# Seven rooms instead of four for gathered expert rows in the dense part

## The chip, the cores and the metric

One NeuronCore of a Trainium2 chip runs the whole kernel as one program. The metric is the device time of one execution in microseconds; for the kernel before, the median of 3 runs is 3912.84 us (3907.16 to 3918.35). The profile is that of one further execution.

## The reference

The kernel computes one decoder block on 1024 tokens of width 1024, in float32. Time mixing and a sparse attention come first; the change touches only the last layer, a product-key expert layer (PEER). Each token picks 128 of 16384 experts (8 heads of 16), with a gate for each. Every expert has a row of 1024 numbers in a table u and one in a table v:

```python
def chunk(args):
    hc, ec, gc = args
    act = jax.nn.gelu(jnp.einsum('cd,chkd->chk', hc, u_tab[ec]), approximate=False) * gc
    return jnp.einsum('chk,chkd->cd', act, v_tab[ec])
```

A residual addition and a layer norm follow and give the output rows.

## The kernel before

The expert layer is done in two ways at once. The last 576 tokens are done **densely**: the dot products of all these tokens with all 16384 experts are formed on TensorE, multiplied by a table of gates that is zero where a token did not pick an expert, and multiplied with v. The first 448 tokens are done by **gather**: for each of their picks the row of u, and later the row of v, is fetched from HBM by an indirect DMA, and VectorE does the arithmetic.

**Dense part.** It starts where the pools of the retrieval close, at the mark `dense`. For 128 groups of 128 experts, `dense_u` forms dot products (or reads those formed earlier back from HBM into `al`), applies GELU on ScalarE, multiplies by the gates `gt` on VectorE (L1317) and splits the product in a high and a low half (L1319) in a tile `A`. `dense_v` multiplies eight such tiles with a tile of v and adds the result to `yacc` on VectorE (L1333). Each tile of u or v comes through `split2`: SyncE's queue loads 128x1024 floats (512 KB) into one of two buffers `raw` (L1270), ScalarE copies them to `whi`, rounded, and GpSimd subtracts to get `wlo` (L1274). I call one such subtraction a **split**. There are 264 of them in the program, numbered here in the order in which they stand on GpSimd, and 48 matrix products or so wait for each. A `raw` buffer is free for the next load when its split has ended.

**Gather.** `peer_gather` goes through 896 rows of work; a row is one indirect DMA that GpSimd issues (L1397), which brings 128x1024 floats (512 KB) into a **room**, and one pass of VectorE over it: L1401 for u (a dot product with the token), L1405 for v (a weighted sum in PSUM). There are four token tiles: three of 256 rows and one of 128 rows. After each, `finish` adds the residual, normalises and writes the output rows. A room is taken again only after VectorE has read it. Rows 1 to 128 use three rooms `g`; rows 129 to 300 (constants `EARLY` and `MIDDLE`) use three `g` and three `gx`; from row 301 on, in the dense part, the rooms are three `g` and `GM` rooms `g2`:

```python
if row >= MIDDLE and row % (GB + GM) >= GB:
    return at["dv"].tile([128, 1024], F32, name="g2", bufs=GM)
return grow()
```

**Order.** The gather's instructions are written last in the source, after the whole dense part. A scheduler merges them in when the program is built: it keeps a model of time, and moves a row forward to where its room is free in that model. The result is one fixed order for each engine; on the chip an engine takes its instructions in that order and waits at the first that is not ready. Rooms therefore decide two things: how many rows may be in flight, and where in the fixed orders of GpSimd and VectorE the rows stand.

Of the kernel before, what the change touches and what calls it, by code (L numbers as in the profile page):

```python
# [41 lines left out]
SQ = 6  # L42
XOB = 2
QIB = 2
GM = 1
FIRST = 3
XR = 3
TIES = 3
# [157 lines left out]
def body(tc, a, out, dbg=None, ntiles=8, mark=lambda s: None):  # L206
# [1129 lines left out]
    def grow(bufs=GB):  # L1336
        return gp.tile([128, 1024], F32, name="g", bufs=bufs)
# [20 lines left out]
    def peer_gather(i, at):  # L1358
# [11 lines left out]
        def room(row):  # L1370
            if EARLY <= row < MIDDLE and row % (GB + XR) >= GB:
                return at["sl"].tile([128, 1024], F32, name="gx", bufs=XR)
# [3 lines that stand above are left out]
# [394 lines left out]
```

## Time and profile before

| | |
|---|---|
| median of 3 runs | 3912.84 us (3907.16 to 3918.35) |
| profiled execution, its time | 3897.85 us |
| its span, first to last instruction | 3895.7 us |
| mean granted TensorE clock | 0.927 of full speed |
| TensorE matmul busy | 3364.8 us (86%) |
| VectorE busy | 2739.8 us (70%) |
| GpSimd busy | 2102.5 us (54%) |
| moved by DMA | 977.19 MB, mean 251 GB/s |

Shares of the whole span mix stages with different limits. Here the end of the program is two stages: the dense part from about 2350 us to about 3600 us, and what is left of the gather after it. The times in the views are microseconds from the start of the span.

### The profile page before, as it was taken

Reading aid. Unit: us, or ns where it says so; the run is one execution under the profiler, and the core shown is the slowest. Engines: PE = TensorE matmul, PEld = TensorE weight load, DVE = VectorE, ACT = ScalarE, POOL = GpSimd, SP = SyncE. Lnnn points to the kernel's source line nnn. Section 1 sums busy time; section 2 is a strip of 40 time slices with the busy share of each in tenths; the row PEclk is TensorE's granted clock in tenths of the full one; section 3 lists DMA queues with packets and bytes.
Section 4 is the critical chain, followed back from the end, with each engine's and each line's share of the span. In section 5 each row is a group of like instructions: output and inputs, shape, how many; then the busy total and the mean of one; then the engine's idle time right before and its main releaser. Section 6 shows DMA issues by size and latency. Waiting matters only on the chain. (4 is left out here: it accounts for less than half of the span.)

```text
span 3895.7 us, 65006 instructions
## 1 busy us (share of the span) xinstructions
PE 3364.8 (86%) x23921; PEld 2994.4 (77%) x23921; DVE 2739.8 (70%) x5625; ACT 1650.8 (42%) x3156; POOL 2102.5 (54%) x1702
## 2 busy tenths in 40 slices
PE   8999998799999999799999989999999999998000
PEld 7677776666777676588999989999999999997000
DVE  7866645856477758899999945666666666676776
ACT  3559842433444443455686683332323222222000
POOL 5442222355555543366565516767766777778554
PEclk9999998899999999899999989999999999998555
DMA  7453335756677665598888749889889888998886
GB/s 230 148 151 104 108 97 178 253 178 224 183 219 220 216 213 159 181 320 297 315 310 313 285 153 314 316 322 339 321 315 319 323 316 326 332 325 300 286 292 230
DMA packets 448418, 977.19 MB, mean 251 GB/s; under 512 B 42036, under 2 KB 190084, under 8 KB 445668
## 3 DMA queue, kind: packets, MB, share of 16 engines
q1 hardware_dynamic: 305060, 488.55, 37.7%
q0 software_dynamic: 143040, 484.50, 35.2%
q8 instruction: 188, 3.08, 0.3%
q14 instruction: 130, 1.06, 0.1%
HBM read 853.88 MB, written 119.01 MB: 250 GB/s over the span
## 5 line engine op out<-in xcount | busy, mean ns | idle before, releaser
L1274 POOL TENSOR_TENSOR wlo<-raw,whi 128x1024 fp32r<-128x1024 f32 x264 | 641.6, 2432 | 333.7 <-ACT whi L235 327.1
L416 POOL TENSOR_TENSOR wlo<-wraw,whi 128x512 fp32r<-128x512 f32 x280 | 370.4, 1325 | 553.8 <-ACT whi L235 511.5
L1397 POOL DMA_INDIRECT g<-in_u_dram,gidx x425 | 434.5, 1022 | 341.7 <-DVE g L1401 211.0
L1405 DVE SCALAR_TENSOR_TENSOR pg<-g,dots,pg 128x1024 f32<-128x1024 f32 x380 | 488.1, 1285 | 158.9 <-DMA g<-in_v_dram,gidx 146.9
L235 ACT ACTIVATE whi<-raw 128x1024 fp32r<-128x1024 f32 x264 | 279.1, 1058 | 632.5 <-PE pair L1289 263.6
L1287 PE MATMUL pair<-A,whi 128*128 128x288 f32 (+2 forms) x2048 | 460.3, 302 | 35.5 <-DVE A L1319 24.4
L1397 POOL DMA_INDIRECT g<-in_v_dram,gidx x384 | 365.8, 953 | 231.3 <-DVE pg L1405 128.3
L1401 DVE SCALAR_TENSOR_TENSOR g<-g,pg 128x1024 f32<-128x1024 f32 x297 | 358.3, 1216 | 161.4 <-DMA g<-in_u_dram,gidx 158.7
L1291 PE MATMUL pair<-h2T,wlo 128*128 128x288 f32 x2048 | 452.5, 301 | 17.2 <-POOL wlo L1274 17.2
L1287 PE MATMUL pair<-h2T,whi 128*128 128x288 f32 x2048 | 451.4, 301 | 18.3 <-ACT whi L235 18.1
L1291 PE MATMUL pair<-A,wlo 128*128 128x288 f32 (+2 forms) x2048 | 458.2, 301 | 4.8 <-POOL wlo L1274 4.8
L1289 PE MATMUL pair<-A,whi 128*128 128x288 f32 (+2 forms) x2048 | 458.4, 301 | 1.9 <-DVE A L1319 1.9
L1289 PE MATMUL pair<-h2T,whi 128*128 128x288 f32 x2048 | 447.7, 300 | 0.0
L1287 PEld LDWEIGHTS pair<-A,whi 128*128 128x128 f32 x2048 | 341.7, 193 | 39.1 <-issue 26.2
L426 PE MATMUL acc<-big,whi 128*128 128x512 f32 x864 | 354.6, 411 | 17.0 <-DVE zs L534 5.9
L1291 PEld LDWEIGHTS pair<-h2T,wlo 128*128 128x128 f32 x2048 | 335.6, 192 | 21.1 <-POOL wlo L1274 20.0
L1287 PEld LDWEIGHTS pair<-h2T,whi 128*128 128x128 f32 x2048 | 335.9, 192 | 20.7 <-ACT whi L235 19.1
L428 PE MATMUL acc<-big,wlo 128*128 128x512 f32 x864 | 349.4, 405 | 2.3 <-POOL wlo L416 2.3
L427 PE MATMUL acc<-big,whi 128*128 128x512 f32 x864 | 347.8, 403 | 1.4 <-DVE big L452 1.4
L1291 PEld LDWEIGHTS pair<-A,wlo 128*128 128x128 f32 x2048 | 341.6, 193 | 5.5 <-POOL wlo L1274 5.5
L1289 PEld LDWEIGHTS pair<-A,whi 128*128 128x128 f32 x2048 | 342.0, 193 | 2.5 <-DVE A L1319 2.5
L1289 PEld LDWEIGHTS pair<-h2T,whi 128*128 128x128 f32 x2048 | 335.8, 192 | 0.7
(489 smaller groups left out, 6632.0 us busy)
## 6 DMA issues: line engine op xcount, KB each, us to landing
raw<-in_vt_dram SPq DMA_DIRECT2D x136, 512.0 KB
raw<-in_ut_dram SPq DMA_DIRECT2D x128, 512.0 KB
wraw<-in_wz_dram SPq DMA_DIRECT2D x152, 256.0 KB
gtD<-st SPq DMA_DIRECT2D x18, 2048.0 KB
gt<-gtD SPq DMA_DIRECT2D x32, 1152.0 KB
dotD<-ds SPq DMA_DIRECT2D x69, 288.0 KB
al<-dotD SPq DMA_DIRECT2D x69, 288.0 KB
mw<-in_wada_dram SPq DMA_DIRECT2D x32, 512.0 KB
```

Of the source, the lines that this page charges most:

```text
L235: copy = lambda o, i, **k: A.activation(o, i, AF.Copy, **k)
L416: G.tensor_tensor(lo, raw, hi.bitcast(F32), op=OP.subtract)
L426: mm(pt, lhsT=wh[:, ks], rhs=ah[:, k, :], start=k == 0, stop=False)
L427: mm(pt, lhsT=wh[:, ks], rhs=al[:, k, :], start=False, stop=False)
L428: ins = mm(pt, lhsT=wl[:, ks], rhs=ah[:, k, :], start=False, stop=k == nk - 1)
L1274: G.tensor_tensor(lo, raw, hi.bitcast(F32), op=OP.subtract)
L1287: mm(pts[n], lhsT=wh, rhs=ah[:, h], start=k == 0, stop=False)
L1289: mm(pts[n], lhsT=wh, rhs=al[:, h], start=False, stop=False)
L1291: latest[:] = [mm(pts[n], lhsT=wl, rhs=ah[:, h], start=False, stop=last)]
L1397: G.indirect_dma_start(out=u, out_offset=None, in_=a["u" if n < halves else "v"], in_offset=bass.IndirectOffsetOnAxis(ap=idx[:, k:k + 1], ...
L1401: V.scalar_tensor_tensor(u, u, 1.0, h2, op0=OP.mult, op1=OP.mult, accum_out=dots[:, k:k + 1])
L1405: V.scalar_tensor_tensor(acc, u, dots[:, k:k + 1], acc, op0=OP.mult, op1=OP.add)
```

## The change

One constant: the dense part's extra rooms `g2` go from one to four, so that with the three rooms `g` there are seven instead of four. The rule of turns (`row % (GB + GM)`) becomes a rule of seven: three rows to `g`, four to `g2`. Nothing else in the source changes, and the instructions are the same in kind and number.

```diff
 QIB = 2
-GM = 1
+GM = 4
 FIRST = 3
```

The scheduler places the rows anew. **GpSimd in the middle of the dense part**, before: a row that names `g_35847` goes to the room `g2` (the listing leaves buffer numbers out of names that repeat), rows that name plain `g` go to the three others, and `x2` means two alike.

```order
L1397 DMA g_35847<-in_u_dram,gidx 128x1024
L1397 DMA g<-in_u_dram,gidx 128x1024 x2
L1274 TENSOR_TENSOR wlo<-raw,whi 128x1024
L1397 DMA g<-in_u_dram,gidx 128x1024
L1397 DMA g_35859<-in_u_dram,gidx 128x1024
L1274 TENSOR_TENSOR wlo<-raw,whi 128x1024
L1397 DMA g<-in_u_dram,gidx 128x1024 x3
L1274 TENSOR_TENSOR wlo<-raw,whi 128x1024
```

The same engine and part of the program with the change:

```order
L1274 TENSOR_TENSOR wlo<-raw,whi 128x1024
L1397 DMA g<-in_u_dram,gidx 128x1024
L1274 TENSOR_TENSOR wlo<-raw,whi 128x1024
L1397 DMA g<-in_u_dram,gidx 128x1024 x2
L1397 DMA g_35925<-in_u_dram,gidx 128x1024
L1397 DMA g_35928<-in_u_dram,gidx 128x1024
L1397 DMA g_35931<-in_u_dram,gidx 128x1024
L1397 DMA g_35934<-in_u_dram,gidx 128x1024
L1274 TENSOR_TENSOR wlo<-raw,whi 128x1024
```

Before, two or three rows stand between two splits; now it is one and six in turn, seven rows for two splits.

**GpSimd at the end of the program**, before. The last rows and the output addition of `finish` (L1427 on `gacc`) end the program; the last split stands some 150 instructions earlier.

```order
L1397 DMA g_36739<-in_v_dram,gidx 128x1024
L1397 DMA g<-in_v_dram,gidx 128x1024 x3
L1397 DMA g_36751<-in_v_dram,gidx 128x1024
L1427 TENSOR_TENSOR gacc<-gacc,gt 64x512 x2
L1766 UNCONDITIONAL_BRANCH
```

With the change, at the same place:

```order
L1397 DMA g_36745<-in_v_dram,gidx 128x1024
L1397 DMA g_36748<-in_v_dram,gidx 128x1024
L1397 DMA g_36751<-in_v_dram,gidx 128x1024
L1274 TENSOR_TENSOR wlo<-raw,whi 128x1024 x6
L1427 TENSOR_TENSOR gacc<-gacc,gt 64x512 x2
L1274 TENSOR_TENSOR wlo<-raw,whi 128x1024 x2
L1427 TENSOR_TENSOR gt<-gt 128x512 x4
L1274 TENSOR_TENSOR wlo<-raw,whi 128x1024
L1427 TENSOR_TENSOR gt<-gt 128x512 x2
L1274 TENSOR_TENSOR wlo<-raw,whi 128x1024 x4
L1427 TENSOR_TENSOR gt<-gt 128x512 x2
```

Row 301 follows split 74 in both orders. Before, row 753 follows split 264, the last, and rows 754 to 896 stand behind it, with the final steps of the dense part among the first of them. Now row 896, the last, follows split 251, and the program ends with the dense part's own output rows. The order on TensorE stays as it was but for a few products that swap places at two borders between `dense_u` and `dense_v`, and for the last tile's small products.

## Rows read from the trace of the kernel before

**Rows 1.** The page: its span, and DMA in 40 equal slices.

```profile
span 3895.7 us, 65006 instructions
DMA  7453335756677665598888749889889888998886
```

**Rows 2.** Busy time by engine, granted clock, DMA share and GB/s in three stretches.

```profile
core 0: us, PE busy (x) PEld busy (x) DVE busy (x) ACT busy (x) POOL busy (x), PEclk, DMA share, GB/s
2350.00:2400.00 50.00, 46.69 (x336) 46.01 (x335) 28.19 (x44) 17.03 (x24) 33.35 (x25) 0.97 0.94 325
2400.00:3600.00 1200.00, 1159.35 (x8498) 1154.36 (x8498) 812.00 (x1041) 345.92 (x437) 858.27 (x625) 0.98 0.89 321
3600.00:3895.70 295.70, 10.36 (x54) 6.90 (x53) 205.10 (x247) 10.23 (x15) 143.99 (x150) 0.51 0.79 268
```

**Rows 3.** Waits from 3640 to 3870 us: total, times, longest.

```profile
POOL g L1397 <- DVE g L1401: 53.7, 62, 4.1
POOL g L1397 <- DVE pg L1405: 41.1, 48, 2.2
DVE g L1401 <- DMA g<-in_u_dram,gidx: 35.6, 47, 4.2
```

**Rows 4.** Line L1397 (a row's issue): two rows of 2350 to 3600, two after.

```profile
L1397 POOL DMA_INDIRECT g<-in_v_dram,gidx x241: 932/940/1226, 2595.0 to 3597.7; - x121
L1397 POOL DMA_INDIRECT g<-in_u_dram,gidx x212: 932/938/1222, 2357.8 to 3305.6; - x106
...
L1397 POOL DMA_INDIRECT g<-in_v_dram,gidx x79: 932/936/1226, 3601.2 to 3868.1; - x79
L1397 POOL DMA_INDIRECT g<-in_u_dram,gidx x64: 932/932/1748, 3641.5 to 3753.4; - x64
```

**Rows 5.** Line L1274 (a split): splits 73 to 264, then the last 13.

```profile
L1274 POOL TENSOR_TENSOR wlo<-raw,whi x192: 2346/2406/2425, 2339.1 to 3598.6; 128x1024 fp32r<-128x1024 f32 x192
...
L1274 POOL TENSOR_TENSOR wlo<-raw,whi x13: 2346/2377/2414, 3530.7 to 3598.6; 128x1024 fp32r<-128x1024 f32 x13
```

**Rows 6.** DMA queues: two rows of 2400 to 3600, one of 3640 to 3870.

```profile
q0 software_dynamic: 62937, 229.17, 50.5%
q1 hardware_dynamic: 103130, 154.99, 38.5%
...
q0 software_dynamic: 18203, 66.31, 84.9%
```

**Rows 7.** Short windows, columns as in rows 2.

```profile
1715.00:1763.00 48.00, 45.97 (x354) 44.85 (x353) 46.12 (x166) 23.22 (x48) 29.73 (x22) 1.00 1.00 377
3344.00:3544.00 200.00, 194.91 (x1418) 193.75 (x1417) 142.09 (x141) 57.17 (x72) 150.16 (x112) 1.00 0.92 330
1500.00:1750.00 250.00, 211.20 (x1156) 180.32 (x1155) 223.88 (x813) 128.35 (x234) 113.69 (x87) 0.90 0.66 221
```

**Rows 8.** VectorE's groups from 2400 to 3600: busy us, mean ns, idle before.

```profile
L1405 DVE SCALAR_TENSOR_TENSOR pg<-g,dots,pg 128x1024 f32<-128x1024 f32 x237 | 304.5, 1285 | 122.6 <-DMA g<-in_v_dram,gidx 112.9 <-issue 7.1 <-DVE pg L1405 0.3
L1401 DVE SCALAR_TENSOR_TENSOR g<-g,pg 128x1024 f32<-128x1024 f32 x199 | 239.5, 1216 | 111.2 <-DMA g<-in_u_dram,gidx 109.3 <-issue 1.3
L1333 DVE SCALAR_TENSOR_TENSOR yacc<-pair,modc,yacc 128x576 f32<-128x576 f32 (+2 forms) x133 | 104.2, 784 | 88.9 <-PE pair L1291 85.3 <-PE pair L1289 1.9 <-issue 1.4
L1317 DVE TENSOR_TENSOR pair<-pair,gt 128x576 f32<-128x576 f32 x118 | 89.6, 760 | 6.7 <-ACT pair L1312 6.2 <-issue 0.3
```

**Rows 9.** Waits from 2400 to 3600 us: total, times, longest.

```profile
ACT whi L235 <- PE pair L1289: 252.5, 83, 6.2
ACT whi L235 <- DMA raw<-in_ut_dram: 128.7, 21, 11.0
ACT whi L235 <- DMA raw<-in_vt_dram: 124.4, 32, 7.7
POOL g L1397 <- issue: 60.0, 248, 0.9
```

**Rows 10.** The chain that ended last, one link; then two output stores by timeline.

```profile
3009.66 12.03 DMA raw<-in_ut_dram
...
3621.36 3.62 SPq L1434 DMA_DIRECT2D out_dram<-gt  x2
3890.30 0.49 SPq L1434 DMA_DIRECT2D out_dram<-gacc  x1
```

## The prediction

> **What bounds the kernel now.** I read the page's slices first, then cut the end of the span into its two stages, then asked in each which wait ends last. The slices show the 16 DMA engines busy at eight or nine tenths from 2337 us to the end [rows 1], but for two different reasons. From 2400 to 3600 us TensorE's matmuls are busy 1159 of 1200 us at a granted clock of 0.98, so the dense part runs at TensorE's pace, with DMA at a share of 0.89 and 321 GB/s beside it [rows 2]. After 3600 us TensorE has done 10 us of work, the clock falls to 0.51, and DMA still moves 268 GB/s: this stage is the rest of the gather [rows 2]. Of the rows of work from 301 on, 453 are issued before 3600 us and 143 after it, the last at 3868.1 us [rows 4]. In the second stage GpSimd waits for VectorE to give a room back (53.7 and 41.1 us), and VectorE waits for a landing (35.6 us for u alone) [rows 3]: four rooms go round one after the other, and 128 rows take 3640 to 3870 us, 1.80 us each.
>
> The pace of the dense part is that of the splits. Splits 73 to 264 start from 2339.1 to 3598.6 us: 191 steps, **6.59 us a split** [rows 5].
>
> **The change part by part.** It adds and removes no instruction. It moves the last 143 rows out of the second stage: 596 rows (301 to 896) now stand between split 74 and split 251, **3.37 rows a split**, where before it was 453 rows in 190 splits, 2.38. The stage behind the dense part goes; the question is what the dense part then costs. I price each engine for one split.
>
> TensorE: 1159.35 us in that stretch over 183 splits, of the 191 steps those that fall in it, are 6.34 us [rows 2]. Nothing is added.
>
> GpSimd: a split is 2.41 us and a row's issue 0.94 [rows 4, 5], with 0.24 us of idle time ahead of it that nothing is named for (60.0 us in 248) [rows 9]. 2.41 + 3.37 x 1.18 = 6.4 us.
>
> VectorE: a row is 1.29 us for v and 1.22 for u, some 1.25; the dense work is 104.2 + 89.6, and a third group, L1319, as large as L1317, over 183 splits: 1.55 us [rows 8]. 1.55 + 3.37 x 1.25 = 5.8 us.
>
> DMA: from 2400 to 3600 us the gather's queue took 50.5% of the engines' time for 229.17 MB, which is 437 rows of 0.524 MB: 606 us, or **1.39 us a row**. After 3640 us it is 84.9% of 230 us for 66.31 MB: 1.54 us a row. SyncE's queue took 38.5% of 1200 us, 462 us over 183 splits: **2.52 us a split** for raw tiles, gates and saved dot products [rows 6]. With 3.37 rows a split that makes 7.2 us at the lower price and 7.7 at the higher, and both are over TensorE's 6.34 and the old pace of 6.59. So the bound of the dense part moves from TensorE to DMA.
>
> How full the engines can be kept is not shown by the trace for such a mix over a long time. The two sides: 1.00 over 48 us in an earlier stage with six rooms, and 0.92 over the fullest 200 us of the dense part, where TensorE was the bound and DMA had no reason to be full [rows 7]. With seven rooms a row that VectorE has not yet read no longer keeps the queue empty, so I take **0.97**: near the first end, less something for the two places where one token tile ends and the next must load its indices, which both lie in this stretch now. For a row I take **1.45 us**, midway between its two prices, since rows will lie closer than in the dense part before and will still be mixed with raw tiles. That is (3.37 x 1.45 + 2.52) / 0.97 = 7.64 us a split. TensorE would be busy 6.34 of 7.64 us, 83%; in a stretch where it was busy 84% the granted clock was 0.90 [rows 7], which would make its work 6.34 x 0.98 / 0.90 = 6.9 us, still below 7.64. So a lower clock costs nothing until DMA is faster than that.
>
> The sum, in the time of the profiled execution: row 301 is issued at 2357.8 us [rows 4]; 177 splits at 7.64 are 1352; from split 251 to split 264 the gather is over, and 13 steps at the 5.66 us that the last 13 splits show (67.9 us in 12 steps) [rows 5] are 74; from split 264 to the store of the dense part's last output rows was 3598.6 to 3625.0, 26 us, and from the store that ends the program to the end of the span 5.4 us [rows 5, 10]. 2358 + 1352 + 74 + 32 = **3816 us**, 80 us less than the span of 3895.7. The profiled execution itself took 3897.85 us, and the median of the runs is 15 us more, so in the terms of the median I take 3912.84 - 80 = **3833 us**, 2.0% less.
>
> The bounds of the two prices: row 1.39 and share 1.00 give 7.20 us a split and 3739 us; row 1.54 and share 0.92 give 8.38 and 3947. No change in time needs 1352 + 80 = 1432 us for 177 splits, **8.09 us a split**, which is the figure on which the sign hangs.
>
> **The rivals.**
>
> *DMA keeps up, and the dense part stays at TensorE's pace.* It would have to move 3.37 x 0.524 + 154.99 / 183 = 2.61 MB in 6.59 us, 397 GB/s. Against it speaks that the fullest 48 us had 377 GB/s with every engine busy [rows 7]. The time would be 2358 + 177 x 6.59 + 106 = 3630 us, or 3647 in the median's terms. The Trainium skill, HBM Reference, section Specifications (TRN2), says that a core streaming alone measures about 425 GB/s, and by that the 397 would be met. The trace does not agree for this mix of transfers: at share 1.00 it has 377. Chance 7%.
>
> *Raw tiles come late, and the dense part slows by more than the tail was worth.* There are only two raw buffers. With the new order a pair of splits stands close, and six rows' issues stand behind it on GpSimd, which takes them in order. The landings of the next two raw tiles fall into that burst. In the dense part before, ScalarE already waited 128.7 and 124.4 us for raw tiles, in 53 of 183 splits [rows 9], and one link of the chain shows 12.03 us from a split's end to the landing [rows 10]. If both tiles of a pair start only when the second split ends and the next pair waits for them, a pair costs the landing, ScalarE's 1.06 us copy, two splits of 2.41 and one row's issue of 0.94: 6.8 us and the landing. Two splits at 8.09 are 16.2 us, so it decides from a landing of 9.4 us on. With 10.2 us a pair is 17.0, a split 8.5, and the time 2358 + 1505 + 106 = 3969 us (3986 by the median); with 12.03 for every pair it would be over 4100. What waits behind is GpSimd's six rows, VectorE's pass over them, and then TensorE. Against it: before, 83 of ScalarE's waits ahead of this copy were for TensorE to release a buffer (252.5 us) [rows 9], so most tiles had landed in time. The Trainium skill, DMA: Bandwidth & Descriptors, section Queues, rings and completion order, says that each DMA engine takes turns between queues packet by packet; by that a longer line of rows would not hold a raw tile back further, and this rival would not come about. The trace leaves that open, since a landing of 12.03 us was seen with four rooms. Chance 17%.
>
> *The rows move and the time does not.* If the engines are kept no fuller than the 0.92 seen, a row at 1.45 makes a split 8.05 us, and the saving is 7 us. Chance 7%.
>
> **How the numbers follow.** My forecast, that DMA becomes the dense part's bound at between 7.2 and 8.0 us a split, has 69%; its own range is 3755 to 3895 us by the median. A change of less than 0.3% (12 us) can't be told from none. Faster by more than that: 69 + 7 = 76%; within it 7%; slower 17%. A range for 8 in 10 takes in the forecast's own, no change, and a little of each side: 3735 to 3945 us.
>
> **What would show it right or wrong.** Right: no row's issue after the last split; the dense part longer, at 7.3 to 7.9 us a split over splits 74 to 251; DMA share 0.95 or more and 340 to 360 GB/s in that stretch; TensorE busy some 83% there with a clock of 0.88 to 0.97; the end within 35 us of the last split. The prediction is wrong if the splits keep to about 6.6 us (DMA can give more than I priced), or go over 8.1 us with DMA at a share below 0.9 (then it is a chain of waits through two raw buffers and not DMA's rate), or if TensorE's clock falls so far that TensorE is the bound again.

## The result, and the profile after

With seven rooms the kernel takes 3788.53 us (median of 4 runs, 3781.83 to 3799.47) against 3910.0 us before on the same chip (median of 4 runs: the three given above, and one of 3889.95 us): a ratio of 0.970, 95% interval 0.966 to 0.974. The medians are 121 us apart; 80 were forecast. The profiled execution has a span of 3786.6 us, 109 us under that of before [rows 1].

The page of the changed kernel, busy time, granted clock and DMA in 40 slices of 95 us:

```profile
span 3786.6 us, 65030 instructions
...
PE   8999999879989999879999998989888898989996
...
PEclk9999998989999999889999999999999999999998
DMA  7453333865677666478888865989989999999994
```

The stage behind the dense part, 296 us with 10 us of TensorE's work [rows 2], is gone. But for the very last, the slices at the end have TensorE, its clock and DMA all high: the gather now runs beside the dense part until 82 us before the end of the span.

The stretch from split 74 to split 251, then two pieces of the end, columns as in [rows 2]:

```profile
2353.50:3697.40 1343.90, 1206.85 (x8518) 1182.40 (x8517) 996.66 (x1263) 345.98 (x444) 985.07 (x770) 0.95 0.95 348
...
3600.00:3700.00 100.00, 90.17 (x650) 87.92 (x649) 79.89 (x76) 24.63 (x31) 81.39 (x65) 1.00 0.98 359
3700.00:3787.00 87.00, 59.52 (x378) 56.53 (x377) 46.06 (x68) 25.83 (x33) 52.59 (x29) 0.85 0.43 150
```

177 splits take 1343.9 us, **7.59 us a split**, against 6.59 before. TensorE is busy 90% of it; it was 97% [rows 2]. DMA's share went from 0.89 to 0.95.

The DMA queues in that stretch, as in [rows 6]; then the issues of rows (L1397) from 2350 us to the end, as in [rows 4]; then the last 14 splits (L1274), as in [rows 5]:

```profile
q0 software_dynamic: 84636, 308.21, 59.6%
q1 hardware_dynamic: 110249, 158.22, 34.9%
```

```profile
L1397 POOL DMA_INDIRECT g<-in_v_dram,gidx x320: 935/941/957, 2548.7 to 3704.6; - x160
L1397 POOL DMA_INDIRECT g<-in_u_dram,gidx x276: 935/941/1823, 2363.3 to 3577.3; - x138
```

```profile
L1274 POOL TENSOR_TENSOR wlo<-raw,whi x14: 2334/2374/3157, 3697.4 to 3763.0; 128x1024 fp32r<-128x1024 f32 x14
```

59.6% of 1343.9 us for 308.21 MB, 588 rows of 0.524 MB, is 1.36 us a row; 34.9% over 177 splits is 2.65 us a split. The last row is issued at 3704.6 us, 58 us ahead of the last split, where before 143 rows came behind it [rows 4].

The waits in the same stretch: total, times, longest; then those of SyncE's own queue.

```profile
ACT whi L235 <- DMA raw<-in_vt_dram: 327.0, 53, 17.7
ACT whi L235 <- DMA raw<-in_ut_dram: 130.0, 28, 15.1
...
DVE g L1401 <- DMA g<-in_u_dram,gidx: 17.7, 13, 7.9
...
DVE pg L1405 <- DMA g<-in_v_dram,gidx: 1.8, 1, 1.8
```

```profile
SPq L1270 <- POOL wlo L1274: 677.5, 153, 12.4
SPq L1310 <- ACT pair L1312: 228.7, 38, 11.3
...
SPq L1723 <- DVE pair L1317: 54.7, 21, 9.5
SPq L1310 <- ACT whi L235: 41.0, 7, 7.7
...
SPq L1310 <- ACT A L235: 21.0, 3, 7.5
```

The same waits of SyncE's queue before, over the same splits (2348.2 to 3518.9 us):

```profile
SPq L1723 <- DVE pair L1317: 97.6, 20, 9.7
...
SPq L1310 <- ACT pair L1312: 21.1, 14, 2.9
```

This is what a reader should stop at. VectorE's waits for rows have all but gone, 19.5 us against 222 before [rows 8]: the rows are there in time. What comes late now are the raw tiles: ScalarE waits 457 us for them, against 253 [rows 9]. They share SyncE's queue with the loads of gates (L1723) and of saved dot products (L1310), and the queue stands 345 us waiting for a buffer of those two, with raw tiles' loads behind: 55 us for gates and 291 for saved dot products, where before it was 98 and 21. So DMA is 95% busy and its most urgent transfers are the late ones.

### The profile page after: what moved, and what is told of

It reads as the page before. It is cut to its first block, busy times and chain, and to the rows that moved or that the text cites. A ratio compares the mean times of both kernels' runs of the same rounds, so it can differ in the third digit from the quotient of the medians.

```text
span 3786.6 us, 65030 instructions
## 1 busy us (share of the span) xinstructions
PE 3412.5 (90%) x23921; PEld 3019.0 (80%) x23921; DVE 2734.4 (72%) x5625; ACT 1649.1 (44%) x3156; POOL 2104.5 (56%) x1702
## 4 chain that ended last, share of the span: by engine, by line
PE 35%; DVE 19%; DMA 13%; POOL 11%; issue 10%; ACT 8%; SPq 1%; POOLq 0%; ACTq 0%; DVEq 0%
POOL g L1397 5%; POOL wlo L1274 4%; DMA raw<-in_vt_dram 4%; PE pair L1291 4%; PE acc L426 4%; PE pair L1287 4%; PE pair L1289 4%; PE acc L427 4%; PE acc L428 4%; DMA raw<-in_ut_dram 3%; ACT gt L235 3%; DVE pg L1405 2%; DMA g<-in_u_dram,gidx 2%; DVE g L1401 2%; PE acc L978 1%
## 5 line engine op out<-in xcount | busy, mean ns | idle before, releaser
L1274 POOL TENSOR_TENSOR wlo<-raw,whi 128x1024 fp32r<-128x1024 f32 x264 | 639.1, 2425 | 297.7 <-ACT whi L235 294.4
L1397 POOL DMA_INDIRECT g<-in_u_dram,gidx x425 | 436.9, 1028 | 311.4 <-DVE g L1401 172.5
L1291 PE MATMUL pair<-A,wlo 128*128 128x288 f32 (+2 forms) x2048 | 466.4, 306 | 51.6 <-POOL wlo L1274 51.3
L1291 PE MATMUL pair<-h2T,wlo 128*128 128x288 f32 x2048 | 462.6, 307 | 45.8 <-POOL wlo L1274 45.7
L1287 PE MATMUL pair<-h2T,whi 128*128 128x288 f32 x2048 | 460.3, 306 | 44.5 <-ACT whi L235 41.3
L1397 POOL DMA_INDIRECT g<-in_v_dram,gidx x384 | 366.2, 954 | 194.7 <-DVE pg L1405 90.8
L1289 PE MATMUL pair<-h2T,whi 128*128 128x288 f32 x2048 | 454.6, 304 | 0.0
L1287 PEld LDWEIGHTS pair<-h2T,whi 128*128 128x128 f32 x2048 | 343.4, 196 | 49.4 <-ACT whi L235 44.3
L1401 DVE SCALAR_TENSOR_TENSOR g<-g,pg 128x1024 f32<-128x1024 f32 x297 | 351.0, 1214 | 17.7 <-DMA g<-in_u_dram,gidx 17.7
L1289 PEld LDWEIGHTS pair<-h2T,whi 128*128 128x128 f32 x2048 | 343.1, 196 | 0.7
```

What stands on the lines that cost most here:

```text
L1274: G.tensor_tensor(lo, raw, hi.bitcast(F32), op=OP.subtract)
L1287: mm(pts[n], lhsT=wh, rhs=ah[:, h], start=k == 0, stop=False)
L1289: mm(pts[n], lhsT=wh, rhs=al[:, h], start=False, stop=False)
L1291: latest[:] = [mm(pts[n], lhsT=wl, rhs=ah[:, h], start=False, stop=last)]
L1397: G.indirect_dma_start(out=u, out_offset=None, in_=a["u" if n < halves else "v"], in_offset=bass.IndirectOffsetOnAxis(ap=idx[:, k:k + 1], ...
L1401: V.scalar_tensor_tensor(u, u, 1.0, h2, op0=OP.mult, op1=OP.mult, accum_out=dots[:, k:k + 1])
```

## The experiments

Every kernel was timed against the kernel before on its own chip, and differences between two of them in us are between medians taken on different chips, good to some 10 us: in these traces split 74 starts anywhere from 2346 to 2372 us with the same work ahead of it, e8 apart. The number for a split is the stretch from split 74 to split 251 over 177, unless it says to split 264 (over 190).

**e1, five rooms; e2, six rooms.** How the time goes with the number of rooms.

```diff
-GM = 4
+GM = 2        # e1; GM = 3 in e2
```

> Five rooms (GM = 2). In the built order 768 rows stand ahead of the last split (753 with four rooms, 896 with seven), 2.46 rows a split, so 128 rows stay behind. Theory DMA rate (the dense part costs whichever is more, TensorE's 6.6 us a split or DMA's rows x 1.36 + 2.65 us at a share near 0.95): demand 6.0 us, so the dense part keeps 6.6 us a split; the tail's rows go at 1.45 to 1.55 us with five rooms instead of 1.80: 3845 to 3865 us, about 1.0 to 1.3% faster than before. Rival, that only the place of the rows in the order counts and not the rooms in flight: the tail's rows stay at 1.80 us and the time is 3875 to 3885 us.

> Six rooms (GM = 3): 849 rows stand ahead of the last split, 2.89 a split, 47 behind it. Theory DMA rate: 2.89 x 1.36 + 2.65 = 6.6 us of DMA work a split, at a share of 0.95 6.9 us, the last split at about 3665 us and 47 rows at 1.5 behind it: 3760 to 3780 us, a little under seven rooms. Rival, late raw tiles by bursts of rows on GpSimd: bursts are shorter than with seven rooms, the split falls to 6.7 us, DMA share under 0.93, and the time is 3715 to 3735 us.

Measured: e1 3858.47 us, ratio 0.986 (0.983 to 0.989); e2 3790.47 us, 0.968 (0.966 to 0.971). The two stretches to split 264, e1 and then e2:

```profile
2362.60:3603.00 1240.40, 1202.34 (x8854) 1195.02 (x8852) 856.46 (x1099) 363.05 (x462) 905.97 (x665) 0.99 0.92 330
```

```profile
2358.00:3681.90 1323.90, 1235.99 (x8862) 1218.02 (x8861) 955.66 (x1257) 369.68 (x469) 983.16 (x746) 0.97 0.94 343
```

With five rooms the dense part keeps TensorE's pace, 6.53 us a split, and the 128 rows behind it go at 1.60 us instead of 1.80 (3613.3 to 3817.7 us). With six it is 6.97 us a split. e1's time is as the DMA theory has it, though its rows behind the dense part cost more than the 1.45 to 1.55 us expected; e2 is 10 us over its range, but far from the rival. Six and seven rooms cannot be told apart.

**e3, seven rooms in the old order.** Rooms and order change together; this takes them apart. Each row's pass on VectorE is tied behind one of the dense part's additions.

```diff
-        V.scalar_tensor_tensor(dst, src, modc[:, 40 + d:41 + d], ...
+        paced.append(V.scalar_tensor_tensor(dst, src, modc[:, 40 + d:41 + d], ...
 def behind(row):
+    if row >= MIDDLE:
+        return tc.issue_after(paced[min((row - MIDDLE) * len(paced) // 453, len(paced) - 1)].ins)
```

> Seven rooms, but the rows' passes on VectorE are tied behind the dense part's additions so that the rows stand as thin as before: 744 rows ahead of the last split, 152 behind it. It separates rooms in flight from the place in the order. Theory DMA rate: the dense part keeps 6.6 us a split, the tail's 152 rows go at 1.45 to 1.55 us: 3855 to 3875 us, 1% faster than before at most. If rooms in flight do nothing: 152 rows at 1.80 us, 3900 to 3915 us. If it comes near seven rooms' 3787 us, the order is not what matters.

Measured: 3869.66 us, ratio 0.988 (0.985 to 0.991). The last 128 rows, with nothing beside them:

```profile
3671.00:3840.00 169.00, 0.00 (x0) 0.00 (x0) 156.13 (x195) 1.83 (x3) 120.24 (x128) 0.50 1.01 393
```

They take 1.32 us each (1.45 to 1.55 was expected), with DMA full at 393 GB/s, where four rooms took 1.80 with the gather's queue at 84.9% [rows 6]: so rooms in flight matter, and the tail's old pace was the turn of four rooms. But with the rows thin in the dense part the gain is 1.2%, and the change's is 3.0%. The larger part comes from where the rows stand.

**e4, the gates' loads by ScalarE's queue.** The same DMA work, but raw tiles no longer queue behind 1.15 MB of gates.

```diff
-                nc.sync.dma_start(gts[i1 // 4], gtD[...
+                nc.scalar.dma_start(gts[i1 // 4], gtD[...
```

> Seven rooms as in the change, but the 1.15 MB loads of gates are issued by ScalarE's queue and not by SyncE's, so that raw tiles no longer stand in line behind them; the work of the DMA engines is the same. Theory DMA rate: 3775 to 3800 us, as with the change. Rival, the raw tiles' lateness sets the pace (ScalarE waited 436 us for raw tiles with the change): these waits fall to half, the split goes from 7.6 to about 7.2 us, and the time to 3705 to 3725 us.

Measured: 3730.38 us, ratio 0.952 (0.950 to 0.955); the change's interval lies wholly above. That is outside both ranges, 5 us above the rival's, and it came by way of a fuller DMA. Its stretch, then issues from 2400 to 3600 us of the change and of e4 (times, KB each, median us to landing):

```profile
2363.80:3640.00 1276.20, 1177.79 (x8487) 1158.19 (x8488) 987.37 (x1264) 345.54 (x444) 980.73 (x769) 0.97 0.98 364
```

```profile
raw<-in_vt_dram SPq DMA_DIRECT2D x111, 512.0 KB, 6.6
gt<-gtD SPq DMA_DIRECT2D x27, 1152.0 KB, 16.4
raw<-in_ut_dram SPq DMA_DIRECT2D x47, 512.0 KB, 7.8
```

```profile
raw<-in_vt_dram SPq DMA_DIRECT2D x117, 512.0 KB, 6.6
gt<-gtD ACTq DMA_DIRECT2D x29, 1152.0 KB, 25.9
raw<-in_ut_dram SPq DMA_DIRECT2D x49, 512.0 KB, 6.5
```

7.21 us a split, DMA at 0.98. The DMA work of a split, share times length over 177, is 0.95 x 7.59 = 7.2 us with the change and 0.98 x 7.21 = 7.1 here: nearly the same work, done in a fuller stretch. The gates, which can wait, land in 25.9 us instead of 16.4. The medians of raw tiles say little: the same 6.6 us for those of v, and for those of u 7.8 and 6.5 here, but 5.8 and 6.5 over the whole stretch (the change first, then e4). What changes is the tile behind a gates' load. Of the landings that the traces show, raw tiles issued within 12 us after such a load took 9.4 us on average with the change (18 tiles, 16.9 at most), the others 5.2 us (31); in e4 it is 7.7 us (30, 10.7 at most) and 5.7 us (59). ScalarE's longest wait for a raw tile falls from 17.7 to 10.2 us and all of these waits from 457 to 377 us, not to half as the rival had it. SyncE's queue still stands 236 us for a buffer of saved dot products.

**e5, gates left out, and e10, copies added.** Both start from e4 and change DMA's work, and with it only ScalarE's issues of these transfers. In e5 the two first tiles of gates are used throughout.

```diff
 def gate_rows(i1):
+    if len(gts) > 1:
+        gts[i1 // 4] = list(gts.values())[i1 // 4 % 2]
+        return
```

> As e4, but 30 of the 32 loads of gates are left out (the first two tiles of gates are used again and again, so the dense tokens' outputs are computed with wrong gates). Instructions and order on the engines stay nearly the same; the DMA engines are spared 30 x 3.9 us, 0.66 us a split. Theory DMA rate: work a split falls from 7.07 to 6.4 us, under TensorE's pace, so the split falls to 6.6 to 6.75 us and the time to 3630 to 3660 us by the median. Rival, the chain through the two raw buffers sets the pace and DMA's share only follows it: 7.1 to 7.2 us a split and 3710 to 3730 us, with the share falling to 0.90.

Its stretch:

```profile
2371.70:3605.40 1233.70, 1164.56 (x8480) 1144.88 (x8481) 981.72 (x1262) 347.80 (x444) 980.22 (x768) 0.99 0.95 347
```

Measured: 3699.8 us, ratio 0.943 (0.941 to 0.946): between the two ranges. Work fell from 7.1 to 6.6 us a split, and the split from 7.21 only to 6.97; TensorE is busy 94% at a clock of 0.99. The queues in e4's stretch, then in e5's (q0 is the gather's, q1 SyncE's, q10 ScalarE's):

```profile
q0 software_dynamic: 84518, 307.79, 62.6%
q1 hardware_dynamic: 37850, 120.36, 25.6%
q10 hardware_dynamic: 69938, 35.56, 9.6%
```

```profile
q0 software_dynamic: 84228, 306.73, 66.6%
q1 hardware_dynamic: 37856, 120.37, 27.6%
```

The gates' queue (q10) gave back 0.69 us a split, as expected, but a row took 1.40 us instead of 1.36 and SyncE's queue 1.92 us a split instead of 1.85: work by share is not quite a fixed price. A first try at adding work, e8, went astray:

```diff
+    for n in range(3):
+        nc.scalar.dma_start(spare[3 * (i1 // 4) + n], a["u"][...
     nc.scalar.dma_start(gts[i1 // 4], gtD[...
```

> As e4, with three copies of 512 KB from HBM to HBM, which nobody reads, issued by ScalarE's queue ahead of each load of gates: about 90 copies in the stretch, at a row's 1.36 us each 0.69 us of DMA work a split more. Theory DMA rate: 7.07 + 0.69 = 7.76 at a share of 0.98, 7.9 us a split, and 3840 to 3870 us. Rival, that DMA's rate is only one of several limits close together and a third of a change in its work shows, as in e5 (0.24 us of 0.66): 7.45 us a split and 3765 to 3785 us.

Measured: 3905.61 us, ratio 0.995 (0.993 to 0.997), for another reason. The row of the copies' line has first and last start at its end:

```profile
L1725 ACTq DMA_DIRECT2D spare<-in_u_dram x96: 496/496/1154, 0.7 to 194.0; - x96
```

Nothing held the copies back, and the scheduler moved them to the program's start, where the first work had to wait: TensorE is busy 22 of the first 100 us, against 82 with the change. It says nothing of the dense part. e10 ties them behind ScalarE's last instruction of `dense_u`, with `tc.issue_after` around the same loop.

> As e8, but each group of three copies is tied behind ScalarE's work in the dense part, since in e8 the scheduler had moved all 96 copies to the first 200 us of the program. About 87 copies of 512 KB in the stretch, at 1.36 us each 0.67 us of DMA work a split more than e4's 7.07. Theory DMA rate: 7.74 at a share of 0.98, 7.9 us a split: 3840 to 3870 us. Rival, several limits close together, a third of a change in the work shows: 7.4 to 7.5 us a split, 3765 to 3785 us.

Measured: 3874.14 us, ratio 0.989 (0.987 to 0.992). Its stretch, and ScalarE's queue in it:

```profile
2355.20:3769.60 1414.40, 1222.37 (x8474) 1201.21 (x8474) 999.87 (x1271) 346.35 (x444) 987.33 (x774) 0.93 0.98 366
```

```profile
q10 hardware_dynamic: 73026, 84.38, 17.2%
```

7.99 us a split, 0.78 more than e4. The queue that carries the copies has 17.2% of 1414.4 us where e4 has 9.6% of 1276.2: 0.68 us more work a split, 0.76 by the share of all queues. Added work shows in full, work taken away shows by half: e4 stands where DMA's rate stops being the only limit. The copies' issues also take 55 us of ScalarE's time, 0.3 us a split; ScalarE waits 412 us for raw tiles meanwhile, but what these issues cost was not tested by itself.

**e6 and e7, the gates by ScalarE's queue with six and with four rooms.**

> Six rooms (GM = 3) and the gates by ScalarE's queue; 847 rows ahead of the last split, 49 behind it. Theory DMA rate: 2.88 x 1.34 + 2.5 = 6.4 us of DMA work a split, so TensorE's 6.65 us a split, the last split at 3625 us, and 49 rows at 1.45 us and the ending behind it: 3715 to 3740 us, the same as e4. Rival, more room is always better: over 3750 us.

> The kernel before with the gates by ScalarE's queue, four rooms: a control. Theory DMA rate with a queue that raw tiles share: where TensorE sets the pace there is little to win, TensorE's idle 41 us of 1200 at most; 3890 to 3912 us. Rival, that the queue is worth its 58 us whatever the rooms: 3850 to 3860 us.

Measured: e6 3763.35 us, 0.960 (0.958 to 0.962); e7 3882.19 us, 0.991 (0.990 to 0.993). Both missed the ranges of the DMA theory, and e6 lies in its rival's. e6 has 6.83 us a split to split 264 where 6.65 was expected, with 49 rows behind, so seven rooms are better than six once the gates are off SyncE's queue. In e7 the split to split 264 falls from 6.58 to 6.38 us: raw tiles' lateness was costing TensorE some 30 us before the change, too. In the trace of e7 ScalarE waits 23 us for raw tiles from split 74 to split 251, and 222 us in that of before. Its ratio says that the queue is worth 34 us with four rooms and, by e4, 58 with seven (68 in the stretch from split 74 to split 251).

**e9, saved dot products by ScalarE's queue as well.**

```diff
-            nc.sync.dma_start(al, dotD[ahead[i1]])
+            nc.scalar.dma_start(al, dotD[ahead[i1]])
```

> As e4, with the loads of saved dot products moved to ScalarE's queue as well, so that SyncE's queue has raw tiles and little else; in e4 it stood 225 us waiting for a buffer of these loads, with raw tiles' loads behind. Theory DMA rate: the share is 0.98 already, so at most 0.1 us a split: 3705 to 3735 us. Rival, raw tiles' lateness is still what holds the pace: the split falls to 6.9 to 7.0 us and the time to 3670 to 3695 us.

Measured: 3778.49 us, ratio 0.963 (0.960 to 0.966): 48 us slower than e4, 41 of them in the stretch, where both theories had it about the same or better. The issue of these loads on ScalarE (min/median/max ns), and a wait of ScalarE, from 2400 to 3600 us:

```profile
L1310 ACTq DMA_DIRECT2D al<-dotD x67: 326/327/8963, 2400.0 to 3596.9; - x67
```

```profile
ACT A L235 <- issue: 60.0, 18, 9.1
```

An issue can hold ScalarE for 9 us; 12 of the 67 took more than 1 us, 68 us together. ScalarE's wait for raw tiles is 263 us in its stretch, less than e4's 377, and the split is longer, 7.44 us. So late raw tiles alone do not set the pace. The 68 us are enough for the loss, and I read it so: an engine with work of its own pays when its issues are held. Why they were held, and whether nothing else is in the 41 us, was not tested.

**e11, three raw buffers.** `RB = 3` on top of e4, and `ALB = 1` for the space.

> As e4, with three raw buffers instead of two and, for their room, one buffer of saved dot products instead of two. The scheduler now puts 778 rows ahead of the last split, 2.5 a split, and 118 behind it. Theory DMA rate: work a split 5.9 us, so TensorE's pace of 6.35 to 6.6 us, the last split at about 3570 to 3615 us and 118 rows at 1.45 us behind it: 3755 to 3810 us. Rival, late raw tiles are what the dense part pays for and where the rows stand matters less: 3690 to 3725 us.

Measured: 3763.61 us, ratio 0.961 (0.959 to 0.963). Waits in the stretch from split 74 to split 264:

```profile
ACT whi L235 <- PE pair L1289: 466.1, 124, 8.3
...
ACT whi L235 <- DMA raw<-in_vt_dram: 17.2, 3, 10.7
```

That is inside the DMA theory's range. Raw tiles are hardly ever late now and ScalarE waits for TensorE; 6.40 us a split. But the scheduler placed only 778 rows ahead of the last split, and 118 come behind it. It is 33 us slower than e4.

## Why the prediction was right, point by point

**The tail was the rows of four rooms, and it goes.** Shown: the last row is issued 58 us ahead of the last split, and e3's row of 1.32 us shows that the rooms' turn, and not DMA or VectorE, had held the tail at 1.80.

**DMA becomes the dense part's bound, between 7.2 and 8.0 us a split.** Right: 7.59, and 7.64 was forecast. e10 shows the mechanism by adding work to e4: 0.7 us more is 0.78 us a split more. With the change itself DMA's rate was not the whole of it: e4 does nearly the same work in 7.21 us. TensorE was forecast busy 83%, and is 90%: 6.8 us a split. The forecast's 6.9 was for a clock of 0.90; at the 0.95 that was granted, its 6.34 would have become 6.5. The 6.34 itself was too low, since the last 13 splits before 3600 us, which have less work, were among its 183. Splits 74 to 251 alone, before, and SyncE's queue there:

```profile
2348.20:3518.90 1170.70, 1145.02 (x8484) 1141.72 (x8484) 786.02 (x1020) 343.24 (x438) 825.70 (x602) 0.99 0.90 323
```

```profile
q1 hardware_dynamic: 109381, 155.66, 39.7%
```

TensorE's work is 6.47 us a split, which at a clock of 0.95 instead of 0.99 is 6.7.

**Its three factors were each a little off, and their errors cancel: that 7.64 lies so near 7.59 is in part luck.** A row cost 1.36 us, not 1.45; it did not become dearer as rows lay closer. SyncE's queue cost 2.65 us a split, not 2.52, and hardly because of the change: in the same splits it was 2.63 before, 39.7% of 1170.7 us. The engines were kept 0.95 full, not 0.97. The reason that I gave for the missing part, the places where one token tile ends, was not the main one: e4 moves nothing but the gates' loads to another queue and has 0.98. Raw tiles behind the gates' loads in SyncE's queue are the missing part.

**The rest of the sum.** In the terms of the forecast, 2358 + 1352 + 74 + 32 = 3816 us, measured 2353.5 + 1343.9 + 65.6 + 23.6 = 3786.6. The last 13 splits and the ending were taken from a trace in which rows still ran beside them; with the gather over they are 17 us shorter, about half in the splits and half in the ending. That is the larger part of the 29 us; that the rows beside them made the difference is not shown by itself. The other part of the difference between 80 and 121 us is the reference: the profiled execution of before was 12 us under the median it is now compared with.

**The rivals.** DMA did not keep up with TensorE's pace: 348 GB/s in the stretch, where 397 were needed. The 377 GB/s that were held against this rival were no ceiling, though: at shares near 1 the traces have from 364 to 411 GB/s. A stretch of the trace before, then one inside e3's last 128 rows:

```profile
1988.00:2000.00 12.00, 11.86 (x94) 11.60 (x93) 11.96 (x27) 9.40 (x21) 9.41 (x6) 1.00 1.01 411
```

```profile
3697.00:3780.00 83.00, 0.00 (x0) 0.00 (x0) 79.37 (x118) 0.26 (x1) 59.01 (x65) 0.50 1.03 410
```

In the dense part's mix the most was 364 GB/s in e4 and 366 in e10, both at a share of 0.98. The Trainium skill's 425 GB/s for a core alone (HBM Reference, Specifications (TRN2)) was reached in no stretch shown here. The second rival named a true mechanism with too high a price: raw tiles did come later, ScalarE's wait for them nearly doubled, and e4 puts a part of it at 58 us, but it did not outweigh the tail. For those 58 us the cause was SyncE's queue and not, as I had it, the bursts of rows on GpSimd, which e4 has too; what the bursts do to the 377 us of waits that e4 still has was not tested. The Trainium skill's rule that a DMA engine takes turns between queues packet by packet (DMA: Bandwidth & Descriptors, Queues, rings and completion order) fits e4: on a queue of its own a gates' load no longer stands whole before a raw tile, which behind it lands in 7.7 us instead of 9.4, and the gates take longer. How the engines choose was not measured by itself.

**What stays open.** With e5's work of 6.6 us a split, TensorE's busy time of 6.6 and a pace of 6.97, no single engine is the bound; several waits of a few us share the rest. I did not take these apart. Nor is it known how much of e4's gain is the sooner landing behind gates, and how much the 55 us that SyncE's queue no longer waits for their buffer. Three raw buffers and rows as dense as with two were not tried together.

## What to carry to other kernels

When the tail of a kernel waits for buffers to turn, more buffers help twice, in the tail itself and by letting the scheduler put the work where another engine was the bound; the second is the larger, and its price is the new bound's work a step, which one can add up beforehand from the shares of the DMA queues. Once DMA is the bound, look at which transfers are urgent and what stands ahead of them in their queue: moving one large, patient load to another engine's queue was worth half as much again as the change itself. Look afterwards at what the scheduler did: buffers that seem unrelated move work, as e11 shows, and a load that nothing holds back is moved itself, as e8 shows.

## What the runs showed of the hardware that was not expected

A load issued from ScalarE took 0.33 us of its time in the median but 8.96 us at worst with the gates' and the dot products' loads both on its queue (e9). Gathered rows of 4 KB pieces alone kept all 16 DMA engines full with seven in flight, at 393 GB/s over 169 us and 410 over 83 of them (e3), and not with four: 66.31 MB in 230 us [rows 6], 288 GB/s.
